# Index scores of all blocks first, three selections side by side, in a decoder with four parallel mixers

## Chip, core and metric

The kernel runs on one core of a Trainium2 chip. The metric is the device time of one launch in microseconds (us). The engines are TensorE (PE; its weight loads are PEld), VectorE (DVE), ScalarE (ACT), GpSimd (POOL) and SyncE (SP), which issues most DMAs. PE runs at one of two clock levels, 1.2 or 2.4 GHz; the granted clock of a stretch is given as a share of the higher one, so 0.5 is all of it at 1.2 GHz.

## What is computed

Two decoder layers act on 512 tokens of width 1024. Each layer normalises its input, projects it for four mixers of 256 columns each (hgrn2, DSA, NSA, mLSTM), puts their outputs side by side, projects them back, and adds the result; a cross-attention and a feed-forward part follow. The change touches the mixer DSA, which picks for every query the 128 keys with the highest index score and attends to these alone:

```python
topk = min(DSA_TOPK_MAX, l_ // 4)
...
    rel = jax.nn.relu(jnp.einsum('bthd,bsd->bhts', iqb, ik))
    score = jnp.einsum('bhts,bth->bts', rel, iwb).astype(F32)
    causal = key_pos[None, :] <= qpos[:, None]
    score = jnp.where(causal[None], score, -jnp.inf)
    _, idx = lax.top_k(score, topk)
    ...
    p = masked_softmax(s, (idx <= qpos[None, :, None])[:, None]).astype(v.dtype)
```

The index has 8 heads of 32 columns. A block is 128 queries; there are four. Block 0 sees 128 keys at most and selects nothing; blocks 1, 2 and 3 see 256, 384 and 512.

## The kernel before, in words

**Stages.** A layer has three stages, each with its own set of PSUM banks. The first holds the index and selection of DSA (`dsa`, L642), NSA with its compression (`nsa`, L1091, `nsa_cmp`, L1164), mLSTM (`ml`, L968), and the projections of all four mixers. The second, which PE opens with L716 (the sums of squares of DSA's latent), holds DSA's attention (`dsa_attn`, L707), hgrn2 (`hg`, L822), and the parts of the output projection (`out_stage`, L1287; its matmuls are those of L329 to L331 with 512 columns). The third holds cross-attention and feed-forward.

**Order.** Each of these is a generator; `weave` and `mix` take the next piece of the one that is least far on, by the costs that each piece yields and a total for each (COST). The program so written goes to a scheduler that orders the instructions of each engine once more, by its own simulation. At run time each engine takes its instructions strictly in that order: one that has to wait holds up all behind it.

**DSA's index and selection.** `index(tb)` (L665) splits a block's queries in two parts (`iqs`, written by ACT and POOL), transposes them on PE (L493, into `iqT`), and for each of 8 heads makes a score on PE (L679, one matmul of up to 512 columns), a relu on ACT (L681, `rel`, 4 buffers), and a row on DVE that adds it, weighted, to the block's scores `iacc` (L684, L685 for the first head, L688 for the others). `select(tb)` (L692) then takes 16 rounds, each of which finds the 8 largest (L696) and overwrites them with a very low number (L697, which the trace shows as a value load and a replace), and at last makes the mask `dmask` (L700) out of what was overwritten. There is one tile `iacc`, so block 2's accumulation comes after block 1's selection, and block 3's after block 2's. All transposes and scores of the index go through one PSUM bank, named `dt`, which NSA's compression and NSA's output (L1161) use as well:

```python
self.banks(banks, "ba", tp=1, sc=2, o=1, dt=1, mb=1)
...
self.alias[id(pd)] = {"tp": "dt", "sc": "dt"}
```

**What hangs on it.** When `dsa` has ended, `hg_space` (L772) closes DSA's memory and opens that of `h_v` and `h_g`, for which `hg_in` (L778) waits; these are hgrn2's last two projections, 192 matmuls of 256 columns (L339 to L341, from `proj_tok`, L476).

**Neighbours in the first stage.** mLSTM's projection chunks are copied to `m_x` (L473) and convolved in DVE rows of 512 columns (L1008, `m_y`, and L1012, `m_th`); its gates go through two scans (L984, L986, on `m_row`). For each of four heads it makes scores in bank `mb` (L1048, triples), multiplies them by a decay on DVE (L1056, `m_p`), multiplies by the values (L1065), and normalises into `mo` (L1069 to L1082, many through the helper on L351). NSA's compression gathers its input in `n_blk` and splits it in two halves of `n_bs` (L1185 and, through L351, the row after it), once for keys and once for values; PE multiplies these with streamed weights (L1192, 64x256). NSA's two attentions use bank `sc` for scores (L552) and `o` for values (L574).

Of the kernel before, what the change touches and what calls it, by code (L numbers as in the profile page):

```python
# [7 lines left out]
FT = mybir.dt.float32  # L8
FR = mybir.dt.float32r
BF = mybir.dt.bfloat16  # L10
U8 = mybir.dt.uint8
AF = mybir.ActivationFunctionType
OP = mybir.AluOpType
AX = mybir.AxisListType

D, S, MEM, DEPTH, FF = 1024, 512, 256, 2, 2816
KC = D // 128
TB = S // 128
# [3 lines left out]
NEG = -1e30  # L22
# [184 lines left out]
class Kernel:  # L207
# [434 lines left out]
    def dsa(self, pool, keep):  # L642
        nc = self.nc
        idx = self.d_idx
        st = self.t(pool, "d_st", [128, 64], bufs=1)

        ik = idx[:, :, 256:288]
        self.sumsq(st[:, 4:8], ik, pool)
        self.rsqrt(pool, st[:, 8:12], st[:, 4:8], 1.0 / 32, EPS)
        self.tt(ik, ik, st[:, 8:12, None].to_broadcast([128, TB, 32]), OP.mult)  # L650
        self.tt(ik, ik, self.row("idxk_gain")[:, None, :].to_broadcast([128, TB, 32]), OP.mult)
        self.rope(idx[:, :, 256:288].rearrange("p t (h d) -> p t h d", h=1), self.ic, self.isn, 4, pool)
        iq = idx[:, :, 0:256].rearrange("p t (h d) -> p t h d", h=8)
        self.rope(iq, self.ic, self.isn, 4, pool)
        iks = self.t2(pool, "iks", [128, TB, 96], FR)
        nc.vector.tensor_copy(iks[:, :, 0:32], ik)
        nc.vector.tensor_copy(iks[:, :, 32:64], ik)
        self.tt(iks[:, :, 64:96], ik, iks[:, :, 0:32].bitcast(FT), OP.subtract)
        ikT = self.t(pool, "ikT", [128, S], FR, bufs=1)
        self.transpose_blocks(ikT[0:96], lambda j: iks[:, j, :].bitcast(FT), TB, nc.vector.tensor_copy, rows=96,  # L660
                              pool=pool)

        yield 4.0

        def index(tb):  # L665
            n = (tb + 1) * 128
            iqs = self.t(pool, "iqs", [128, 8, 96], FR, bufs=1)
            nc.scalar.activation(iqs[:, :, 0:32], iq[:, tb], AF.Copy)
            nc.scalar.activation(iqs[:, :, 64:96], iq[:, tb], AF.Copy)
            self.tt(iqs[:, :, 32:64], iq[:, tb], iqs[:, :, 0:32].bitcast(FT), OP.subtract, nc.gpsimd)  # L670
            iqT = self.t(pool, "iqT", [128, 8, 128], FR, bufs=1)
            for g in range(2):
                self.transpose_blocks(iqT[0:96, 4 * g:4 * g + 4].rearrange("p a b -> p (a b)"),
                                      lambda j: iqs[:, 4 * g + j, :].bitcast(FT), 4, self.act_copy, rows=96,
                                      pool=pool)
            acc = self.t(pool, "iacc", [128, S], bufs=1)[:, :n]
            for h in range(8):
                sc = self.psum("sc", pool=pool)
                nc.tensor.matmul(sc[:, :n], iqT[0:96, h], ikT[0:96, :n], start=True, stop=True)  # L679
                rel = self.t2(pool, "rel", [128, S])  # L680
                nc.scalar.activation(rel[:, :n], sc[:, :n], AF.Relu, scale=1.0 / 16)  # L681
                w = idx[:, tb, 288 + h:289 + h]
                if h == 0:
                    nc.vector.tensor_scalar(acc[:, :n - 128], rel[:, :n - 128], w, None, op0=OP.mult)  # L684
                    nc.vector.scalar_tensor_tensor(acc[:, n - 128:n], rel[:, n - 128:n], w, self.k("neg"),  # L685
                                                   op0=OP.mult, op1=OP.add)
                else:
                    nc.vector.scalar_tensor_tensor(acc, rel[:, :n], w, acc, op0=OP.mult, op1=OP.add)  # L688
                yield 0.7
            return acc  # L690

        def select(tb, acc, masks):  # L692
            n = (tb + 1) * 128
            m8 = self.t(pool, "m8", [128, 8])
            for r in range(16):
                nc.vector.max(m8, acc)  # L696
                nc.vector.match_replace(acc, m8, acc, -3e38)  # L697
                yield 0.4 + 0.25 * tb
            masks[tb] = self.t(keep, f"dmask{tb}", [128, n], BF, bufs=1)
            nc.vector.tensor_scalar(masks[tb], acc, -2e38, NEG, op0=OP.is_gt, op1=OP.mult)  # L700

        masks = self.d_masks = {0: None}
        for tb in range(1, TB):
            acc = yield from index(tb)
            yield from select(tb, acc, masks)

    def dsa_attn(self, pool):  # L707
        nc, l = self.nc, self.l
# [828 lines left out]
    def run(self):  # L1537
        nc = self.nc
        late = ExitStack()
        for l in range(DEPTH):  # L1540
# [8 lines left out]
            right, index = ExitStack(), ExitStack()  # L1549
            self.hqf = self.pool(right, "hgqf", side="right")  # L1550
            self.mo = {2: self.t(self.mp, "mo2", [128, 2, S], bufs=1), 3: self.t(self.mp, "mo3", [128, TB, 256], bufs=1)}
            pd = self.pool(index, "dsa", n2=4, n4=0, side="right")
            self.alias[id(pd)] = {"tp": "dt", "sc": "dt"}
            acc = self.dsa_in(pd)
            if l == 0:
# [44 lines left out]
            with ExitStack() as e:  # L1600
                p = self.pool(e, "xa")
# [29 lines left out]
```

## Time and profile before

| | before |
|---|---|
| median of 3 runs | 1687.93 us (1684.38 to 1699.76) |
| profiled execution | 1688.9 us |
| its span | 1687.1 us |
| PE busy | 1607.5 us, 95% |
| DVE, ACT, POOL busy | 924.0, 712.5, 799.1 us |
| mean granted clock of PE | 0.972 |

The profile is of one execution. "Busy" of PE counts a matmul from start to end, at whichever clock it ran. A row of a timeline gives start, duration, engine, line, operation, tiles (output <- inputs), sizes, and in brackets the engine's idle time ahead of it and what ended that. Layer 0's first stage ends at about 268 us, layer 1's at about 1115 us.

### The profile page before, as it was taken

Reading aid. Unit: us, or ns where it says so; the run is one execution under the profiler, and the core shown is the slowest. Engines: PE = TensorE matmul, PEld = TensorE weight load, DVE = VectorE, ACT = ScalarE, POOL = GpSimd, SP = SyncE. Lnnn points to the kernel's source line nnn. Section 1 sums busy time; section 2 is a strip of 40 time slices with the busy share of each in tenths; the row PEclk is TensorE's granted clock in tenths of the full one; section 3 lists DMA queues with packets and bytes.
Section 4 is the critical chain, followed back from the end, with each engine's and each line's share of the span. In section 5 each row is a group of like instructions: output and inputs, shape, how many; then the busy total and the mean of one; then the engine's idle time right before and its main releaser. Section 6 shows DMA issues by size and latency. Waiting matters only on the chain.

```text
span 1687.1 us, 25484 instructions
## 1 busy us (share of the span) xinstructions
PE 1607.5 (95%) x9256; PEld 1333.1 (79%) x9262; DVE 924.0 (55%) x1760; ACT 712.5 (42%) x1525; POOL 799.1 (47%) x698
## 2 busy tenths in 40 slices
PE   7899998998899989999999999989998999999999
PEld 7778877777788868888898887677877888888887
DVE  5697688876755330344225884879786644123420
ACT  5555453454654443443324433423665433223321
POOL 5664333456448888874412010144672344444442
PEclk9999997999999999999999999979999999999999
DMA  5342212212338999953355734122131233333331
GB/s 160 89 119 76 70 34 84 57 38 85 112 121 286 305 316 319 333 192 93 105 156 178 262 107 132 58 95 57 45 119 38 66 97 90 92 100 94 94 103 66
DMA packets 114365, 212.72 MB, mean 126 GB/s; under 512 B 12984, under 2 KB 30136, under 8 KB 114240
## 3 DMA queue, kind: packets, MB, share of 16 engines
q1 hardware_dynamic: 111888, 206.11, 38.7%
q10 hardware_dynamic: 2032, 3.94, 0.7%
q8 instruction: 73, 1.20, 0.3%
q0 software_dynamic: 320, 1.05, 0.2%
q14 instruction: 52, 0.43, 0.1%
HBM read 170.69 MB, written 40.35 MB: 125 GB/s over the span
## 4 chain that ended last, share of the span: by engine, by line
PE 84%; DVE 8%; issue 3%; DMA 2%; POOL 2%; ACT 2%; SPq 0%; POOLq 0%; ACTq 0%; DVEq 0%
PE acc L329 14%; PE acc L331 14%; PE acc L330 14%; PE sc L330 5%; PE sc L331 5%; PE sc L329 5%; PE acc L339 3%; PE acc L340 3%; PE acc L341 3%; PE hb L856 3%; PE o L574 2%; PE sc L552 2%; PE tp L493 2%; PE mb L1048 1%; PE dt L493 1%
## 5 line engine op out<-in xcount | busy, mean ns | idle before, releaser
L293 POOL TENSOR_TENSOR wl<-wr,wh 128x512 fp32r<-128x512 f32 (+5 forms) x432 | 551.7, 1285 | 459.3 <-ACT wh L292 447.8
L292 ACT ACTIVATE wh<-wr 128x512 fp32r<-128x512 f32 (+5 forms) x432 | 252.1, 592 | 336.2 <-PE acc L330 149.2
L329 PE MATMUL acc<-xh,wh 128*128 128x512 f32 (+1 forms) x704 | 276.9, 395 | 0.8 <-ACT xh L1283 0.5
L330 PE MATMUL acc<-xl,wh 128*128 128x512 f32 (+1 forms) x704 | 274.6, 390 | 2.9 <-DVE xl L1277 2.9
L331 PE MATMUL acc<-xh,wl 128*128 128x512 f32 (+1 forms) x704 | 275.4, 392 | 0.4 <-POOL wl L293 0.4
L466 DVE TENSOR_TENSOR xT<-acc,xT 128x512 f32<-128x512 f32 (+1 forms) x112 | 68.1, 611 | 214.4 <-PE acc L331 213.6
L329 PEld LDWEIGHTS acc<-xh,wh 128*128 128x128 f32 x704 | 133.9, 191 | 32.1 <-issue 1.7
L330 PEld LDWEIGHTS acc<-xl,wh 128*128 128x128 f32 x704 | 134.3, 191 | 30.8 <-DVE xl L1277 4.0
L331 PEld LDWEIGHTS acc<-xh,wl 128*128 128x128 f32 x704 | 134.1, 190 | 28.7 <-POOL wl L293 1.1
L329 PE MATMUL acc<-f_gh,wh 128*128 128x512 f32 x352 | 139.1, 397 | 6.8 <-ACT f_gh L1491 6.8
L339 PE MATMUL acc<-wh,xh 128*128 128x256 f32 (+2 forms) x480 | 140.6, 296 | 4.9 <-DMA wh<-whl 3.8
L331 PE MATMUL acc<-f_gh,wl 128*128 128x512 f32 x352 | 139.7, 398 | 0.7 <-POOL wl L293 0.7
L330 PE MATMUL sc<-xl,wh 128*128 128x512 f32 x352 | 139.7, 397 | 0.0
L330 PE MATMUL acc<-f_gl,wh 128*128 128x512 f32 x352 | 139.5, 398 | 0.0
L340 PE MATMUL acc<-wl,xh 128*128 128x256 f32 (+2 forms) x480 | 139.0, 291 | 0.0
L331 PE MATMUL sc<-xh,wl 128*128 128x512 f32 x352 | 139.0, 395 | 0.0
L329 PE MATMUL sc<-xh,wh 128*128 128x512 f32 x352 | 138.0, 393 | 0.0
L341 PE MATMUL acc<-wh,xl 128*128 128x256 f32 (+2 forms) x480 | 137.4, 288 | 0.0
L318 POOL TENSOR_TENSOR phl<-pr,phl 128x512 fp32r<-128x512 f32 (+3 forms) x72 | 95.1, 1321 | 35.0 <-ACT phl L317 31.8
L317 ACT ACTIVATE phl<-pr 128x512 fp32r<-128x512 f32 (+3 forms) x72 | 44.2, 613 | 133.9 <-DMA pr<-in_wst 117.2
L339 PEld LDWEIGHTS acc<-wh,xh 128*128 128x128 f32 x480 | 92.9, 194 | 8.8 <-DMA wh<-whl 4.3
L340 PEld LDWEIGHTS acc<-wl,xh 128*128 128x128 f32 x480 | 93.3, 195 | 1.4 <-issue 0.8
(407 smaller groups left out, 3159.8 us busy)
## 6 DMA issues: line engine op xcount, KB each, us to landing
wr<-in_wst SPq DMA_DIRECT2D x332, 256.0 KB, 2.7
whl<-phl SPq DMA_DIRECT2D x52, 512.0 KB, 3.9
pr<-in_wst SPq DMA_DIRECT2D x52, 256.0 KB, 4.1
wh<-whl SPq DMA_DIRECT2D x52, 256.0 KB, 4.1
wl<-whl SPq DMA_DIRECT2D x52, 256.0 KB, 4.4
wr<-in_wst SPq DMA_DIRECT2D x48, 128.0 KB, 2.2
wr<-in_wst SPq DMA_DIRECT2D x32, 192.0 KB, 2.4
whl<-phl SPq DMA_DIRECT2D x8, 524.0 KB, 3.7
```

The source lines that it names most:

```text
L292: nc.scalar.activation(hi, raw, AF.Copy)
L293: nc.gpsimd.tensor_tensor(lo, raw, hi.bitcast(FT), op=OP.subtract)
L318: nc.gpsimd.tensor_tensor(both[:, 1], raw, both[:, 0].bitcast(FT), op=OP.subtract)
L329: self.nc.tensor.matmul(acc, wh, xh, start=(j == 0), stop=False)
L330: self.nc.tensor.matmul(acc, wh, xl, start=False, stop=False)
L331: self.nc.tensor.matmul(acc, wl, xh, start=False, stop=(j == n - 1))
L339: self.nc.tensor.matmul(acc, xh[:, s], wh, start=(first and j == 0), stop=False)
L340: self.nc.tensor.matmul(acc, xh[:, s], wl, start=False, stop=False)
L341: self.nc.tensor.matmul(acc, xl[:, s], wh, start=False, stop=(last and j == n - 1))
L466: self.nc.vector.tensor_add(self.xT[c][:, cols], acc, self.xT[c][:, cols])
L493: self.nc.tensor.transpose(p[:rows, j * 128:j * 128 + 128], src(j), self.ident)
L856: nc.tensor.matmul(sc[s0:s1, b + t0:b + t1], kk[po:po + 64, b + s0:b + s1], qq[po:po + 64, b + t0:b + t1], start=True, stop=True)
```

## The change

All three index passes come first, each into a tile of its own (`iacc1`, `iacc2`, `iacc3`); then 16 times a round of block 1, one of block 2 and one of block 3; then the three masks. The queries are split and transposed in two halves of four heads (`iqs` with one buffer, `iqT` with two, each half the size), and the pool's buffers for `rel` go from 4 to 3. In the new code lines from L665 on have other numbers: score L682, accumulation L687 to L691, maximum L700, replace L701, mask L706, and all that lies behind it stands one line further down (L1193 for L1192, L717 for L716).

```diff
+        accs = {tb: self.t(pool, f"iacc{tb}", [128, (tb + 1) * 128], bufs=1) for tb in range(1, TB)}
+
         def index(tb):
             n = (tb + 1) * 128
-            iqs = self.t(pool, "iqs", [128, 8, 96], FR, bufs=1)
...
-            iqT = self.t(pool, "iqT", [128, 8, 128], FR, bufs=1)
+            acc = accs[tb]
             for g in range(2):
...
-            acc = self.t(pool, "iacc", [128, S], bufs=1)[:, :n]
-            for h in range(8):
...
-        def select(tb, acc, masks):
-            n = (tb + 1) * 128
-            m8 = self.t(pool, "m8", [128, 8])
-            for r in range(16):
-                nc.vector.max(m8, acc)
-                nc.vector.match_replace(acc, m8, acc, -3e38)
+
+                four = iq[:, tb, 4 * g:4 * g + 4]
+                iqs = self.t(pool, "iqs", [128, 4, 96], FR, bufs=1)
+                nc.scalar.activation(iqs[:, :, 0:32], four, AF.Copy)
+                nc.scalar.activation(iqs[:, :, 64:96], four, AF.Copy)
+                self.tt(iqs[:, :, 32:64], four, iqs[:, :, 0:32].bitcast(FT), OP.subtract, nc.gpsimd)
+                iqT = self.t(pool, "iqT", [128, 4, 128], FR, bufs=2)
...
+                for h in range(4 * g, 4 * g + 4):
+                    sc = self.psum("sc", pool=pool)
+                    nc.tensor.matmul(sc[:, :n], iqT[0:96, h % 4], ikT[0:96, :n], start=True, stop=True)
+                    rel = self.t2(pool, "rel", [128, S])
...
+                    yield 0.7
+
+        for tb in range(1, TB):
+            yield from index(tb)
+
+        for r in range(16):
+            for tb in range(1, TB):
+                m8 = self.t(pool, f"m8{tb}", [128, 8])
+                nc.vector.max(m8, accs[tb])
+                nc.vector.match_replace(accs[tb], m8, accs[tb], -3e38)
                 yield 0.4 + 0.25 * tb
-            masks[tb] = self.t(keep, f"dmask{tb}", [128, n], BF, bufs=1)
-            nc.vector.tensor_scalar(masks[tb], acc, -2e38, NEG, op0=OP.is_gt, op1=OP.mult)
-
         masks = self.d_masks = {0: None}
         for tb in range(1, TB):
-            acc = yield from index(tb)
-            yield from select(tb, acc, masks)
+            masks[tb] = self.t(keep, f"dmask{tb}", [128, (tb + 1) * 128], BF, bufs=1)
+            nc.vector.tensor_scalar(masks[tb], accs[tb], -2e38, NEG, op0=OP.is_gt, op1=OP.mult)
...
-            pd = self.pool(index, "dsa", n2=4, n4=0, side="right")
+            pd = self.pool(index, "dsa", n2=3, n4=0, side="right")
```

What the scheduler makes of it shows in the order of the built programs. On PE, in layer 0, a score of block 3 (`dt<-ikT,iqT 128x512`) stood among the projections' matmuls of 512 columns before. Here is the first of the eight:

```order
L330 MATMUL acc<-xl,wh 128x512
L679 MATMUL dt<-ikT,iqT 128x512
L331 MATMUL acc<-xh,wl 128x512
L329 MATMUL acc<-xh,wh 128x512
L330 MATMUL acc<-xl,wh 128x512
L331 MATMUL acc<-xh,wl 128x512
L329 MATMUL acc<-xh,wh 128x512
```

Now the eight stand in this place, ahead of NSA's first compressed keys (`n_hid`):

```order
L493 MATMUL dt<-kc,iqs 96x128 x4
L574 MATMUL o<-PT,n_tok 64x128 x4
L682 MATMUL dt<-ikT,iqT 128x512
L993 MATMUL mb<-kc,m_row 128x4 x4
L682 MATMUL dt<-ikT,iqT 128x512 x2
L993 MATMUL mb<-kc,m_row 128x4 x4
L682 MATMUL dt<-ikT,iqT 128x512
L493 MATMUL dt<-kc,iqs 96x128 x4
L682 MATMUL dt<-ikT,iqT 128x512 x4
L1201 MATMUL dt<-kc,n_hid 128x64 x2
L521 MATMUL tp<-kc,qd 128x128 x4
L1209 MATMUL dt<-n_w_1098,n_hT 128x64 x2
```

All eight scores of block 3 follow one another within seven rows, with transposes and 128x4 matmuls of mLSTM's gates between them, and eleven rows further down begins NSA's second compression (L1193). Before, the eight were spread over some 150 rows.

On DVE, in layer 0, block 1's last rounds, its mask (`dmask`) and the second pass of `n_bs`, which PE's second compression reads, stood so:

```order
L697 MATCH_REPLACE iacc<-m_830,iacc 128x256
L351 TENSOR_TENSOR n_blk<-n_blk,cols 128x16x31
L696 MAX m_830<-iacc 128x8
L1185 CAST n_bs<-n_blk 128x16x32
L697 MATCH_REPLACE iacc<-m_830,iacc 128x256
L351 TENSOR_TENSOR n_bs<-n_blk,n_bs 128x16x32
L700 TENSOR_SCALAR dmask_1180<-iacc 128x256
L473 TENSOR_TENSOR m_x<-acc,R 128x512
```

And now so, where `iacc_571` is block 2's tile and `iacc_572` is block 3's:

```order
L691 SCALAR_TENSOR_TENSOR iacc_572<-rel,d_idx,iacc_572 128x512
L700 MAX m_1923<-iacc_571 128x8
L1013 SCALAR_TENSOR_TENSOR m_th<-m_th,m_y 128x512
L351 TENSOR_TENSOR n_blk<-n_blk,cols 128x16x31
L700 MAX m_1371<-iacc_572 128x8
L701 MATCH_REPLACE iacc_571<-m_1923,iacc_571 128x384
L351 TENSOR_TENSOR ql<-tp,qh 128x512
L1211 COPY n_cmp_1323<-dt 128x64
L1186 CAST n_bs<-n_blk 128x16x32
L701 MATCH_REPLACE iacc_572<-m_1371,iacc_572 128x512
L700 MAX m_2012<-iacc_571 128x8
L351 TENSOR_TENSOR n_bs<-n_blk,n_bs 128x16x32
```

The row that finishes `n_bs` has moved from one row ahead of block 1's mask to 55 rows behind it (that mask is 45 rows ahead of the first row shown); conv rows, accumulations of blocks 2 and 3 and rounds of both now stand between.

On PE, at the end of layer 0's first stage, mLSTM's last head stood so before:

```order
L1048 MATMUL mb<-m_hi_2749,m_hi_2803 128x512
L1048 MATMUL mb<-m_lo,m_hi_2803 128x512
L1048 MATMUL mb<-m_hi_2749,m_lo 128x512
L1048 MATMUL mb<-m_hi_2749,m_hi_2803 128x384
L1048 MATMUL mb<-m_lo,m_hi_2803 128x384
L1048 MATMUL mb<-m_hi_2749,m_lo 128x384
L1161 MATMUL dt<-n_eT,n_vbd 128x512
L1048 MATMUL mb<-m_hi_2749,m_hi_2803 128x256
L1048 MATMUL mb<-m_lo,m_hi_2803 128x256
L1048 MATMUL mb<-m_hi_2749,m_lo 128x256
L1048 MATMUL mb<-m_hi_2749,m_hi_2803 128x128
L1048 MATMUL mb<-m_lo,m_hi_2803 128x128
L1048 MATMUL mb<-m_hi_2749,m_lo 128x128
```

Now, for two of its triples:

```order
L1049 MATMUL mb<-m_hi_2800,m_hi_2859 128x384
L1049 MATMUL mb<-m_lo,m_hi_2859 128x384
L1049 MATMUL mb<-m_hi_2800,m_lo 128x384
L329 MATMUL acc<-xh,wh 128x512
L330 MATMUL acc<-xl,wh 128x512
L331 MATMUL acc<-xh,wl 128x512
L329 MATMUL acc<-xh,wh 128x512
L330 MATMUL acc<-xl,wh 128x512
L331 MATMUL acc<-xh,wl 128x512
L1049 MATMUL mb<-m_hi_2800,m_hi_2859 128x256
L1049 MATMUL mb<-m_lo,m_hi_2859 128x256
L1049 MATMUL mb<-m_hi_2800,m_lo 128x256
```

Before, nothing but one matmul of NSA stood among the triples of L1048; now matmuls of the output stage (512 columns) stand between them, and hgrn2's projections (256 columns) ahead of them. In all 144 matmuls of 256 columns and 12 of 512 that stood behind the second stage's first matmul (L716, now L717) in layer 0 stand ahead of it now, and 96 and 12 in layer 1.

## Rows read from the trace of the kernel before

**Rows 1.** The page, part 1: busy time of each engine, share of the span, instructions.

```profile
PE 1607.5 (95%) x9256; PEld 1333.1 (79%) x9262; DVE 924.0 (55%) x1760; ACT 712.5 (42%) x1525; POOL 799.1 (47%) x698
```

**Rows 2.** Table by stretches: length, busy us by engine, granted clock, DMA share, GB/s.

```profile
240.00:275.00 35.00, 26.98 (x162) 20.01 (x162) 32.55 (x84) 10.73 (x27) 3.09 (x3) 0.74 0.03 8
275.00:310.00 35.00, 31.22 (x213) 28.00 (x212) 28.43 (x53) 12.95 (x27) 22.34 (x28) 0.87 0.40 124
1085.00:1110.00 25.00, 17.62 (x112) 14.64 (x110) 24.66 (x66) 6.28 (x16) 1.34 (x2) 0.74 0.00 1
1110.00:1130.00 20.00, 16.21 (x117) 15.75 (x117) 12.18 (x20) 5.65 (x12) 12.32 (x18) 0.82 0.56 185
110.00:130.00 20.00, 16.21 (x125) 14.37 (x125) 19.90 (x32) 11.59 (x28) 13.39 (x9) 0.91 0.49 146
310.00:410.00 100.00, 99.68 (x768) 82.48 (x770) 72.74 (x149) 50.05 (x129) 54.95 (x61) 1.00 0.18 52
950.00:970.00 20.00, 18.95 (x146) 16.19 (x145) 16.00 (x37) 8.75 (x23) 0.73 (x1) 0.91 0.77 263
1130.00:1250.00 120.00, 119.06 (x881) 98.09 (x883) 96.42 (x197) 59.48 (x152) 68.03 (x72) 1.00 0.20 58
```

**Rows 3.** PE's timeline, end of layer 0's first stage: start, us, operation, [idle <-releaser].

```profile
258.77 2.08 PE L1161 MATMUL dt<-n_eT,n_vbd 128*128 128x512 f32 x2 [0.69 <-DVE mo L351]
...
272.57 1.08 PE L1281 MATMUL tp<-kc,mo 128*128 128x128 f32 x4 [2.54 <-DVE mo L351]
```

**Rows 4.** DVE's timeline in the same stretch: block 3's rounds and its mask.

```profile
266.06 0.69 DVE L696 MAX8 m<-iacc 128x8 f32<-128x512 f32 x1
...
267.58 0.69 DVE L696 MAX8 m<-iacc 128x8 f32<-128x512 f32 x1
...
274.08 0.43 DVE L700 TENSOR_SCALAR dmask<-iacc 128x512 bf16<-128x512 f32 x1
```

**Rows 5.** PE's timeline, 291 to 297.5 us: first and last of 43 matmuls.

```profile
291.89 0.28 PE L339 MATMUL acc<-wh,xh 128*128 128x256 f32 x1
...
296.86 0.28 PE L339 MATMUL acc<-wh,xh 128*128 128x256 f32 x1
```

**Rows 6.** DVE's timeline, 110 to 118 us: n_bs, block 1's mask, mlstm's scans.

```profile
110.51 1.35 DVE L351 TENSOR_TENSOR n_bs<-n_blk,n_bs 128x512 fp32r<-128x512 f32 x1
111.78 0.28 DVE L700 TENSOR_SCALAR dmask<-iacc 128x256 bf16<-128x256 f32 x1
...
114.52 1.18 DVE L984 TENSOR_TENSOR_SCAN m_row<-one,m_row 4x512 f32<-4x512 f32 x1
...
117.47 2.17 DVE L986 TENSOR_TENSOR_SCAN m_row<-zero,m_row 4x512 f32<-4x512 f32 x1
```

**Rows 7.** Tile view of iacc: durations ns min/median/max, first and last start, forms.

```profile
L696 DVE MAX8 m<-iacc x96: 397/561/696, 79.5 to 1108.4; 128x8 f32<-128x256 f32 x32, 128x8 f32<-128x384 f32 x32, 128x8 f32<-128x512 f32 x32
L697 DVE MATCH_VALUE_LOAD iacc<-m,iacc x96: 60/92/93, 82.1 to 1109.1; 128x8 f32 x96
L697 DVE MATCH_REPLACE8 iacc<-m,iacc x96: 397/543/678, 82.2 to 1109.2; 128x256 f32<-128x256 f32 x32, 128x384 f32<-128x384 f32 x32, 128x512 f32<-128x512 f32 x32
L688 DVE SCALAR_TENSOR_TENSOR iacc<-rel,d_idx,iacc x42: 466/742/1772, 54.9 to 1078.4; 128x256 f32<-128x256 f32 x14, 128x384 f32<-128x384 f32 x14, 128x512 f32<-128x512 f32 x14
```

**Rows 8.** Line view of L1008, mlstm's convolution (columns as in rows 7).

```profile
L1008 DVE SCALAR_TENSOR_TENSOR m_y<-m_x,cols,m_y x24: 731/752/1872, 122.2 to 1065.9; 128x512 f32<-128x512 f32 x24
```

**Rows 9.** PE's timeline, 64 to 67 us: two scores of block 1.

```profile
64.86 0.28 PE L679 MATMUL dt<-ikT,iqT 96*128 96x256 f32 x1
...
66.21 0.28 PE L679 MATMUL dt<-ikT,iqT 96*128 96x256 f32 x1
```

**Rows 10.** Tile view of rel: what ScalarE's relu waited for (us, times).

```profile
  PE dt L679: 30.5, 20
```

**Rows 11.** PE's timeline: second stage's first matmul, and hgrn2's last transposes.

```profile
268.23 1.81 PE L716 MATMUL dt<-one,ckvsq 128*128 128x1 f32 x8
...
414.54 0.69 PE L1281 MATMUL tp<-kc,h_g 128*128 128x128 f32 x2 [2.17 <-DVE h_g L351]
```

More of the change, by code (lines that the diff above doesn't have):

```diff
@@ L663, in dsa @@
         yield 4.0
+        accs = {tb: self.t(pool, f"iacc{tb}", [128, (tb + 1) * 128], bufs=1) for tb in range(1, TB)}
         def index(tb):
             n = (tb + 1) * 128
-            iqs = self.t(pool, "iqs", [128, 8, 96], FR, bufs=1)
-            nc.scalar.activation(iqs[:, :, 0:32], iq[:, tb], AF.Copy)
-            nc.scalar.activation(iqs[:, :, 64:96], iq[:, tb], AF.Copy)
-            self.tt(iqs[:, :, 32:64], iq[:, tb], iqs[:, :, 0:32].bitcast(FT), OP.subtract, nc.gpsimd)
-            iqT = self.t(pool, "iqT", [128, 8, 128], FR, bufs=1)
@@ L672, in index @@
-            for g in range(2):
-                self.transpose_blocks(iqT[0:96, 4 * g:4 * g + 4].rearrange("p a b -> p (a b)"),
-                                      lambda j: iqs[:, 4 * g + j, :].bitcast(FT), 4, self.act_copy, rows=96,
-                                      pool=pool)
-            acc = self.t(pool, "iacc", [128, S], bufs=1)[:, :n]
-            for h in range(8):
[L678 to L689, printed above, removed]
@@ L690, in index @@
-            return acc
-        def select(tb, acc, masks):
-            n = (tb + 1) * 128
-            m8 = self.t(pool, "m8", [128, 8])
-            for r in range(16):
-                nc.vector.max(m8, acc)
-                nc.vector.match_replace(acc, m8, acc, -3e38)
+            acc = accs[tb]
+            for g in range(2):
+                four = iq[:, tb, 4 * g:4 * g + 4]
[4 more added lines that the diff above has]
+                iqT = self.t(pool, "iqT", [128, 4, 128], FR, bufs=2)
+                self.transpose_blocks(iqT[0:96].rearrange("p a b -> p (a b)"), lambda j: iqs[:, j, :].bitcast(FT), 4,
+                                      self.act_copy, rows=96, pool=pool)
+                for h in range(4 * g, 4 * g + 4):
+                    sc = self.psum("sc", pool=pool)
+                    nc.tensor.matmul(sc[:, :n], iqT[0:96, h % 4], ikT[0:96, :n], start=True, stop=True)
+                    rel = self.t2(pool, "rel", [128, S])
+                    nc.scalar.activation(rel[:, :n], sc[:, :n], AF.Relu, scale=1.0 / 16)
+                    w = idx[:, tb, 288 + h:289 + h]
+                    if h == 0:
+                        nc.vector.tensor_scalar(acc[:, :n - 128], rel[:, :n - 128], w, None, op0=OP.mult)
+                        nc.vector.scalar_tensor_tensor(acc[:, n - 128:n], rel[:, n - 128:n], w, self.k("neg"),
+                                                       op0=OP.mult, op1=OP.add)
+                    else:
+                        nc.vector.scalar_tensor_tensor(acc, rel[:, :n], w, acc, op0=OP.mult, op1=OP.add)
+                    yield 0.7
```

## Prediction

> **What bounds the kernel now.** I read the page first: TensorE (PE) is busy 95% of the span, the vector engine (DVE) 55%, ScalarE 42%, GpSimd 47% [rows 1]. So the time is PE's work plus what PE loses, and PE loses in two ways: it waits, or it runs at 1.2 instead of 2.4 GHz (a granted clock of 0.74 over 35 us is 35 x 0.26 x 2 = 18 us at the lower level). The table by stretches [rows 2] shows where. In the long middles (as 310 to 410 and 1130 to 1250 us) PE is full and at 2.4 GHz. It loses where the first stage of a layer ends: 8.0 of 35 us idle at 240 to 275 and 3.8 more up to 310, then in layer 1 7.4 of 25 us at 1085 to 1110 and 3.8 more up to 1130. In the same stretches DVE is 93% and 99% busy. The timelines say with what: PE stands at matmuls that wait for DVE to make nsa's and mlstm's outputs (mo) [rows 3], and on DVE the rounds of block 3's selection (maximum, value load, replace: 1.52 us from one maximum to the next) stand between these rows, until the mask is made at 274.08 us [rows 4]. The stall is short of covering work, too: hgrn2's projections, which are free of all this, stand behind it in PE's order.
>
> **What the change moves.** The order of the built program shows three things.
>
> First, block 3's selection leaves the end. Its mask is made some 100 DVE rows earlier, and 48 triples of hgrn2's projection matmuls (144) and 12 matmuls of the output stage now stand in front of the matmul L717 that opens the second stage, as fill between mlstm's last scores. By the spacing of such matmuls (0.118 us for 256 columns, 42 of them from the first row to the last [rows 5], and twice that for 512) that is 144 x 0.118 + 12 x 0.23 = 19.8 us of PE work; in layer 1 96 and 12, 14.1 us.
>
> Second, a new stall comes into the middle of the first stage. The eight scores of block 3 follow one another in PE's order with nearly nothing between, and the next matmuls of any length, nsa's second compression (L1193), read n_bs, which DVE now makes 55 rows behind dmask of block 1, where before it stood just ahead of that mask (110.51 and 111.78 us [rows 6]). PE takes its matmuls in order, so it can't pass L1193 before DVE has gone through those rows. Their sum in layer 0, by the rows of before: two accumulations of 384 columns at 0.60 (between the least, 0.47, and the median, 0.74) and eight of 512 at 0.74: 7.1; 13 selection instructions of block 2 at 0.56 (maximum) and 0.63 (load and replace) and one round of block 3 at 1.52: 9.2 [rows 4, 7]; six of conv's m_y at 0.75 [rows 8], and two m_th at 0.7 as an estimate from these: 5.9; mlstm's two scans at 1.2 and 2.2 [rows 6] with three more rows of 512 columns at 0.67: 5.4; nsa's n_blk, n_bs, ql, n_hs and small rows, an estimate from n_bs: 7.5. Together 35.1, less 0.08 us each because a row starts before the one ahead has ended (110.51 + 1.35, next at 111.78 [rows 6]): 56 x 0.08 = 4.5. So some 30 us. PE's own work in that stretch, counted from the order (from block 2's seventh score to L1193) at the spacings above and at 0.15 us for a transpose, is 10 us with its waits for hand-overs. PE loses about 21 us. At 110 to 130 it lost 3.8 us before, and some 1.5 us to the clock [rows 2]; hence 16 us more. After such a wait PE restarts at 1.2 GHz, as it does behind the stall at the stage's end (clock 0.87 over 275 to 310 [rows 2]): 3 us of work at that level takes 1.5 us more. In layer 1 the mask of block 1 stands behind the last accumulation of block 2, so the stretch is 41 rows and 22 us by the same prices, PE's work in it 8 us, and 950 to 970 lost some 2 us before: 12 us more, and 1.5 at the restart.
>
> Bounds of the stall. Below: were DVE free, a score would only wait for its bank, which ScalarE's relu has to empty; the closest two scores of before are 1.35 us apart [rows 9], eight are 11 us, no more than PE's own work and what it lost there before. Above: the conv and accumulate rows reach 1.77 and 1.87 us when GpSimd works beside them, while the selection rows never pass 0.70 [rows 7, 8]; 15 such rows at 1 us more make it 15 us longer in layer 0, where GpSimd is 67% busy at 110 to 130, and nothing in layer 1, where it is 4% [rows 2]. I take the value without it, since a PE that stands still frees no weight buffers and gives GpSimd little to split.
> The Trainium skill ("Perfetto Trace Analysis", section "Optimizing Tensor Performance") wants independent matmul groups to rotate through PSUM banks so that the emptying of one overlaps the next. These 24 scores have one bank, before and after; the trace agrees so far that ScalarE's relu waited 20 times for a score [rows 10]. By the rule alone the new stall would be the 11 us of the lower bound, which is the second rival.
>
> Third, stage two begins later and with less fill. L717 comes 20 us of moved work plus the new stall later, less what the end of stage one gives back. Behind it stand fewer matmuls by just the moved 19.8 us, so PE as such loses nothing; but the chains of hgrn2 and of dsa's attention (146 us from 268.23 to 414.54 [rows 11]) ran beside those matmuls, and DVE has 73 to 97 us of work in each 100 to 120 us of it [rows 2]. Where the shorter stretch is too short for the chain, PE waits. Between nothing (the chain shrinks as PE's queue does) and all of 19.8 + 14.1 = 34 us I take 5, near the lower end, because PE, not DVE, was the full engine there.
>
> **Small parts, costed at nothing.** iqs and iqT are made in halves: 12 more ScalarE and 6 more GpSimd instructions, each of half the size, on engines 42% and 47% busy [rows 1]. Three relu buffers in place of four: accumulation h - 3 instead of h - 4 must be done before relu h; in the early blocks it was. If that cover is gone, it lies inside the new stall, which DVE sets anyway. The count of DVE and PE instructions is the same. No DMA is added.
>
> **The sum, against the profiled execution (1688.9 us; its span is 1687.1, the median of the runs 1687.93).** Layer 0: new stall +16, restart +1.5. End of stage one: 240 to 310 lost 8.0 + 3.8 idle, and of 27 us at 1.2 GHz (0.74 and 0.87 [rows 2]) some 16 were busy, 8 us too many: 20 in all. What stays: the last head's scores, mask multiplies and the transposes that wait for mo are still a chain, with 39 fills of 0.12 to 0.23 us between; I keep 6 us. So -14. Layer 1: +12, +1.5; 11.2 idle and 20 us at 1.2 GHz, 9 of them busy, 4.5: 16 in all, 4 stay: -12. Less fill in stage two: +5. Sum: 16 + 1.5 - 14 + 12 + 1.5 - 12 + 5 = +10. I go to 1700, a point above, as the new stalls are counted row by row while what the stage's end gives back is estimated.
>
> **Rivals.** (a) Slower: stage two is bound by its chain. Place: PE at hb, sc and dt matmuls between L717 and the transposes of h_g. It decides from the point where PE is idle there for over 10% of the stretch. For it: the chain starts some 30 us later in layer 0 and keeps its DVE work of 100 us. Against: PE was 99.7% busy at 310 to 410 [rows 2], so the chain had waited for PE. Price: half of the 34 us instead of 5, +12, and with the GpSimd contention in the first stall another 8: 1720. (b) Faster: the new stall is only the bank's hand-over (11 us, hidden by PE's work and what was lost there before), and the end of both stages gives back its 26 us: +3 - 26 + 5 = -18, 1671. For it: the rows counted in front of n_bs need not start late; those that wait for nothing on PE (conv, block 2's rounds) may run while PE is still at work ahead of the scores. Against: DVE was 99.5% busy at 110 to 130 already [rows 2], so it has no time in hand there. (c) The selections don't run side by side as the words say: block 1's sixteen rounds are through before block 2's first, and only blocks 2 and 3 alternate. That is what the order shows; the time still depends on where the rounds stand, not on their turns, so this alone is 1689.
>
> **Chances.** The forecast, 1700 with a range of its own from 1689 to 1712: 0.50. Rival (a): 0.21. Rival (b): 0.22. Rival (c): 0.07. About 1% (17 us) is what a measurement of this kernel can tell from no change. Slower by more than that, over 1705: most of (a), 0.18, and three tenths of the forecast, 0.15: 0.33. Faster, under 1671: half of (b) and what lies beyond it, 0.14. The rest, 0.53, lies within 1%. The range from 1669 to 1721 leaves out a tenth at either end: the outer halves of (a) and of (b).
>
> **What would show it.** Right: a dip of PE and of its clock at some 115 to 145 and 950 to 980 us with DVE full, the eight scores of block 3 there one accumulation apart, block 3's mask at about 185 instead of 274 us, fill matmuls between mlstm's last scores, and the dips at 255 to 275 and 1090 to 1110 mostly gone. Wrong: no dip in the middle (then (b)), or the dips at the end gone and PE idle by over 10 us more between L717 and h_g's transposes (then (a)).

## The result and the profile after

| | before | after |
|---|---|---|
| median | 1686.66 us (4 runs) | 1709.97 us (4 runs, 1704.78 to 1718.87) |
| ratio of the two | | 1.014 (95% interval 1.0109 to 1.0172) |
| profiled execution, its span | 1688.9, 1687.1 us | 1713.6, 1711.8 us |
| mean granted clock of PE | 0.972 | 0.961 |

The change makes the kernel 1.4% slower; its profiled execution is 3.6 us above its median. The page, part 1, which answers to [rows 1], shows PE 14 us busier although its work is the same: part of it ran at the lower clock. DVE is 14 us less busy.

```profile
PE 1621.5 (95%) x9256; PEld 1340.7 (78%) x9262; DVE 910.4 (53%) x1760; ACT 715.1 (42%) x1537; POOL 799.9 (47%) x704
```

The table by stretches of the kernel after, as [rows 2] for before (length, busy us of PE, PEld, DVE, ACT, POOL, granted clock, DMA share, GB/s):

```profile
100.00:160.00 60.00, 45.23 (x281) 33.43 (x280) 59.01 (x145) 34.74 (x86) 28.27 (x24) 0.77 0.26 78
160.00:298.00 138.00, 137.55 (x930) 113.99 (x928) 69.70 (x153) 61.12 (x134) 50.23 (x39) 1.00 0.23 65
298.00:340.00 42.00, 35.75 (x194) 28.49 (x193) 35.87 (x74) 13.33 (x30) 23.00 (x28) 0.96 0.33 105
340.00:375.00 35.00, 35.00 (x177) 29.46 (x177) 22.98 (x55) 9.14 (x25) 11.14 (x15) 0.56 0.03 8
375.00:429.00 54.00, 52.32 (x461) 43.65 (x463) 38.60 (x84) 31.42 (x84) 32.97 (x37) 1.00 0.14 40
955.00:1000.00 45.00, 32.41 (x167) 21.92 (x166) 43.91 (x102) 22.43 (x55) 6.38 (x8) 0.66 0.20 64
1100.00:1147.00 47.00, 46.93 (x355) 40.45 (x355) 17.05 (x32) 19.49 (x44) 14.05 (x11) 1.00 0.22 74
1147.00:1170.00 23.00, 18.22 (x91) 14.99 (x91) 20.02 (x43) 6.44 (x12) 13.12 (x21) 0.78 0.38 126
```

There are two dips in the middle of the first stages (100 to 160, 955 to 1000), with DVE full. The ends of these stages (160 to 298, 1100 to 1147) are without any loss now. The second stage of layer 0 has 35 us in which PE is never idle and yet runs at 1.2 GHz nearly throughout (340 to 375).

Put as losses, where a loss is PE's idle time plus, for each us, busy time times (1 - granted clock):

| stretch (us in before; after) | before | after | change |
|---|---|---|---|
| layer 0, start (0 to 100; 0 to 100) | 21.4 | 22.1 | +0.7 |
| first stage's middle (100 to 160; same) | 5.5 | 22.5 | +17.0 |
| its rest (160 to 268.2; 160 to 298.0) | 9.3 | 0.4 | -8.9 |
| second stage (to 414.5; to 429.1) | 16.9 | 24.8 | +7.9 |
| third stage, start of layer 1 (to 889.6; to 922.3) | 21.8 | 18.1 | -3.7 |
| layer 1, first stage's middle (120 us each) | 7.5 | 24.1 | +16.6 |
| its rest (to 1114.6; to 1147.3) | 12.2 | 0.1 | -12.1 |
| second stage (to 1244.2; to 1268.9) | 6.8 | 12.6 | +5.8 |
| rest | 15.9 | 15.0 | -0.9 |

The sum, +22.4, is most of the 24.7 us by which the spans differ.

What PE waits for in the new dip is in its timeline of layer 0 (columns as in [rows 3]; the last three rows are of the second stage):

```profile
117.58 0.49 PE L682 MATMUL dt<-ikT,iqT 96*128 96x512 f32 x1 [0.32 <-ACT iqT L497]
...
125.92 0.79 PE L682 MATMUL dt<-ikT,iqT 96*128 96x512 f32 x1 [0.68 <-ACT iqT L497]
127.40 0.79 PE L682 MATMUL dt<-ikT,iqT 96*128 96x512 f32 x1 [0.69 <-ACT rel L684]
129.45 0.80 PE L682 MATMUL dt<-ikT,iqT 96*128 96x512 f32 x1 [1.26 <-ACT rel L684]
131.00 0.80 PE L682 MATMUL dt<-ikT,iqT 96*128 96x512 f32 x1 [0.76 <-ACT rel L684]
132.48 0.47 PE L1201 MATMUL dt<-kc,n_hid 64*128 64x64 f32 x2 [0.69 <-ACT rel L684]
137.64 1.09 PE L521 MATMUL tp<-kc,qd 128*128 128x128 f32 x4 [4.69 <-DVE n_hs L351]
...
143.94 1.12 PE L574 MATMUL o<-PT,n_tok 128*64 128x128 f32 x8 [0.23 <-ACT PT L497]
144.85 1.07 PE L605 MATMUL tp<-kc,stat 128*64 128x128 f32 x8
145.85 0.48 PE L1193 MATMUL acc<-wh,n_bs 128*64 128x256 f32 x1
...
297.99 1.00 PE L717 MATMUL dt<-one,ckvsq 128*128 128x1 f32 x8
...
339.60 0.39 PE L552 MATMUL sc<-kst,qh 128*128 128x256 f32 x1 [0.95 <-ACT P L560]
...
429.08 0.38 PE L1282 MATMUL tp<-kc,h_g 128*128 128x128 f32 x2
```

A score takes 0.79 us at 1.2 GHz, then PE waits 0.69 us until ScalarE's relu has emptied the bank, then comes the next: 1.48 us a score, against which a matmul of that size among others takes 0.23 us of PE ([rows 5], twice the spacing). The eight and the transposes between them fill 117.6 to 132.5. The longest wait follows, 4.69 us for DVE, at the transposes of qd, NSA's queries (L521); the profile puts it down to n_hs, and the row ahead of n_hs makes qd itself. Of the 14.6 us of waits that the timeline lists between 100 and 160 us, 4.9 are for a relu that empties the bank, 1.0 for iqT, 6.9 for DVE (n_hs, 1.59 at m_row, 0.66 at spread) and 1.8 for NSA's softmax on ScalarE (P, PT).

At L1193, where the prediction put the stall, PE doesn't wait at all. DVE's timeline shows why: the row that finishes n_bs is made 2.0 us before PE gets there. It shows, too, what the wait at L521 was: from 105.15 us on no row of DVE has an idle time noted ahead of it (31.7 of 32.0 us busy from 105.66 to 137.63), and qd and n_hs stand behind these rows. Block 3's mask, 274.08 us in [rows 4], is there at 185.22:

```profile
105.15 1.37 DVE L691 SCALAR_TENSOR_TENSOR iacc<-rel,d_idx,iacc 128x384 f32<-128x384 f32 x1 [0.51 <-ACT rel L684]
...
134.66 2.58 DVE L1181 COPY n_blk<-n_kv 64x496 f32<-64x496 f32 x2
137.27 0.23 DVE L1128 COPY qd<-n_qr 128x128 f32<-128x128 f32 x1
137.41 0.22 DVE L351 TENSOR_TENSOR n_hs<-dt,n_hs 128x64 f32<-128x64 f32 x1
...
143.16 0.67 DVE L351 TENSOR_TENSOR n_bs<-n_blk,n_bs 128x512 fp32r<-128x512 f32 x1
...
185.22 0.43 DVE L706 TENSOR_SCALAR dmask<-iacc 128x512 bf16<-128x512 f32 x1
```

In the kernel before, the same row of qd stood ahead of block 1's mask (111.78 us [rows 6]):

```profile
106.84 0.23 DVE L1127 COPY qd<-n_qr 128x128 f32<-128x128 f32 x1
```

The tile view of rel, which answers to [rows 10], has 26 waits of the relu for a score in place of 20, and below them the scores that wait for a relu:

```profile
  PE dt L682: 30.7, 26
...
  PEld dt L682: 16.8, 14
  PE dt L682: 11.2, 12
```

The last three rows of PE's timeline answer to [rows 11]: the second stage runs from 297.99 to 429.08 us, 131.1 us in place of 146.3. The wait at 339.60 is the last before the clock falls; none follows while it is low.

### The profile page after: what moved, and what is told of

The parts are those of the page before. It is cut to its first block, busy times and chain, and to the rows that moved or that the text cites. A ratio compares the mean times of both kernels' runs of the same rounds, so it can differ in the third digit from the quotient of the medians.

```text
span 1711.8 us, 25529 instructions
## 1 busy us (share of the span) xinstructions
PE 1621.5 (95%) x9256; PEld 1340.7 (78%) x9262; DVE 910.4 (53%) x1760; ACT 715.1 (42%) x1537; POOL 799.9 (47%) x704
## 3 DMA queue, kind: packets, MB, share of 16 engines
q10 hardware_dynamic: 2032, 3.94, 0.7%
## 4 chain that ended last, share of the span: by engine, by line
PE 67%; DVE 8%; POOL 2%; ACT 2%; issue 2%; DMA 1%; SPq 0%; POOLq 0%; ACTq 0%; DVEq 0%
PE acc L329 12%; PE acc L330 12%; PE acc L331 12%; PE sc L330 5%; PE sc L331 5%; PE sc L329 5%; PE acc L339 2%; PE acc L340 2%; PE acc L341 2%; PE hb L857 2%; PE tp L493 1%; PE o L574 1%; PE sc L552 1%; PE mb L1049 1%; PE acc L1193 1%
## 5 line engine op out<-in xcount | busy, mean ns | idle before, releaser
L293 POOL TENSOR_TENSOR wl<-wr,wh 128x512 fp32r<-128x512 f32 (+5 forms) x432 | 546.1, 1273 | 487.8 <-ACT wh L292 458.7
L331 PE MATMUL acc<-xh,wl 128*128 128x512 f32 (+1 forms) x704 | 271.4, 386 | 0.0
```

The source lines that it names most:

```text
L293: nc.gpsimd.tensor_tensor(lo, raw, hi.bitcast(FT), op=OP.subtract)
L331: self.nc.tensor.matmul(acc, wl, xh, start=False, stop=(j == n - 1))
```

## The experiments

The theory after the first trace: scores that stand close together in PE's order pass through their one bank at the pace of a score and a relu, and PE, which takes its matmuls in order, can do nothing else meanwhile; and the second stage, with 20 us of fill taken out of it, loses PE's clock. The rivals: DVE's queue sets the pace of the stall; the turns of the rounds cost; the small parts cost. All ratios are against the kernel before, run beside; the losses are those of each version's profiled execution.

**E1, selections one after another.** All index passes first, then each block's 16 rounds and its mask.

```diff
-        for r in range(16):
-            for tb in range(1, TB):
...
+        def select(tb):
...
+            for r in range(16):
...
+            yield from index(tb)
+        for tb in range(1, TB):
+            yield from select(tb)
```

> The changed kernel, but each block's 16 rounds and its mask come in one piece, block after block; all index passes still come first. Theory (where the scores of block 3 stand sets the time, not the turns of the rounds): within 0.4% of the changed kernel, 1704 to 1716 us, with the same stalls at 115 to 145 and 960 to 1000 us. Rival (taking the rounds in turn is what costs): back to 1684 to 1692 us.

Measured: 1711.44 us, 1.0143 (1.0094 to 1.0193); 22.5 and 22.0 us lost in the two middles. The theory's number: the turns of the rounds are worth nothing.

**E2, the small parts alone.** The kernel before with `iqs` and `iqT` in halves and three buffers for `rel`.

```diff
-            iqs = self.t(pool, "iqs", [128, 8, 96], FR, bufs=1)
+                iqs = self.t(pool, "iqs", [128, 4, 96], FR, bufs=1)
...
-            pd = self.pool(index, "dsa", n2=4, n4=0, side="right")
+            pd = self.pool(index, "dsa", n2=3, n4=0, side="right")
```

> The kernel before (one tile for the scores, index and selection block by block) with the queries split in halves of four heads and three relu buffers. Theory: these small parts cost nothing, 1682 to 1692 us, no stall at 115 to 145 us. Rival (three relu buffers or the halves hold PE up): over 1697 us.

Measured: 1687.57 us, 1.0008 (0.999 to 1.0025). They cost nothing.

**E3, two banks for the scores.** The changed kernel, with DSA's scores in the two banks of NSA's.

```diff
-            self.alias[id(pd)] = {"tp": "dt", "sc": "dt"}
+            self.alias[id(pd)] = {"tp": "dt"}
```

> The changed kernel with DSA's scores in the two banks that NSA's scores use in place of the one bank they share with NSA's compression; the transposes stay where they were. If the one bank sets the pace of block 3's scores (1.48 us each: a score at 1.2 GHz and a relu), the loss at 100 to 160 us falls from 22 to under 10 us and the time to 1685 to 1697 us. If DVE's queue does (DVE 100% busy there), the loss stays over 16 us and the time at 1702 to 1715 us.

Measured: 1673.51 us, 0.9917 (0.9896 to 0.9939), below both expected ranges and faster than the kernel before. Its table by stretches and two of block 3's scores in PE's timeline:

```profile
100.00:160.00 60.00, 56.85 (x413) 47.25 (x412) 59.77 (x143) 35.37 (x84) 37.60 (x29) 1.00 0.40 116
```

```profile
103.64 0.39 PE L682 MATMUL sc<-ikT,iqT 96*128 96x512 f32 x1
103.86 0.28 PE L1193 MATMUL acc<-wh,n_bs 128*64 128x256 f32 x1
103.98 0.39 PE L682 MATMUL sc<-ikT,iqT 96*128 96x512 f32 x1
```

DVE is busy 59.8 of 60 us, more than in the stall, and PE loses 3.2 us, so a full DVE by itself doesn't hold PE up. The two scores shown start 0.34 us apart, with no wait for a relu. But with the other bank the scheduler also wrote another order: the eight scores stand at 84.7 to 116.0 us, most of them apart, and on DVE qd and the second n_bs, for which the prediction and the trace of the changed kernel had PE waiting, are made 21 and 20 us earlier:

```profile
116.10 0.23 DVE L1128 COPY qd<-n_qr 128x128 f32<-128x128 f32 x1
...
123.64 0.67 DVE L351 TENSOR_TENSOR n_bs<-n_blk,n_bs 128x512 fp32r<-128x512 f32 x1
```

So bank, place of the scores and DVE's order changed together here.

**E4, index of block 3 behind selection 1.** Separate tiles, one bank.

```diff
-        for tb in range(1, TB):
-            yield from index(tb)
+        yield from index(1)
+        for tb in range(1, TB):
+            if tb < TB - 1:
+                yield from index(tb + 1)
+            yield from select(tb)
```

> Separate tiles, but index of block 3 is written behind the selection of block 1 (index 1, index 2, selection 1, index 3, selection 2, selection 3). In PE's order four of block 3's scores stand where all eight stood, four some 30 us of PE work later; the second stage's first matmul stands within 1.5 us of PE work of where the change put it. Theory (packing the scores makes the stall): the new stalls halve, 17 and 20 us to about 8 each, and the time is 1685 to 1697 us. Rival (the second stage with less fill is what costs): 1702 to 1715 us.

Measured: 1683.43 us, 0.9986 (0.997 to 1.0001). The middles lose 11.5 and 10.9 us where the changed kernel lost 22.5 and 24.1. Against the kernel before (5.5 and 7.5) the stall is 6.0 and 3.4 us in place of 17.0 and 16.6: more than half of it goes, in the same single bank. The time is a little under the theory's range. The halving that the theory wanted was not tested, as the trace has no four scores together. In layer 0 block 3's first four stand behind the second compression, 1.6 to 6.3 us apart, the others from 171.1 to 181.8 us, and PE waits at none of them:

```profile
134.51 0.40 PE L682 MATMUL dt<-ikT,iqT 96*128 96x512 f32 x1
136.07 0.39 PE L682 MATMUL dt<-ikT,iqT 96*128 96x512 f32 x1
138.40 0.48 PE L682 MATMUL dt<-ikT,iqT 96*128 96x512 f32 x1
144.71 0.40 PE L682 MATMUL dt<-ikT,iqT 96*128 96x512 f32 x1
```

What is left in this middle is therefore not the bank's, and here, too, DVE makes qd and the second n_bs 16 us earlier than in the changed kernel (121.37 and 127.53 us).

**E5, four rounds of sixteen.** The changed kernel with a quarter of the rounds.

```diff
-                nc.vector.max(m8, accs[tb])
-                nc.vector.match_replace(accs[tb], m8, accs[tb], -3e38)
+                if r < 4:
+                    nc.vector.max(m8, accs[tb])
+                    nc.vector.match_replace(accs[tb], m8, accs[tb], -3e38)
```

> The changed kernel with 4 of the 16 rounds of each selection (12 are left out, so more keys stay selected in the sense of the mask; the rest is computed as before). PE's order around block 3's scores stays as in the changed kernel, DVE has about 13 rounds fewer in the stretch. If the single bank sets the pace, the eight scores stay 1.4 to 1.5 us apart and of the 17 and 20 us lost in the middle at least 11 stay in each layer: 1695 to 1712 us. If DVE's queue does, the scores close up, the middle loses under 8 us and the time falls to 1670 to 1688 us.

Measured: 1731.94 us, 1.0254 (1.0225 to 1.0282). The scores in PE's timeline:

```profile
127.73 0.79 PE L682 MATMUL dt<-ikT,iqT 96*128 96x512 f32 x1 [0.68 <-ACT iqT L497]
...
131.07 0.79 PE L682 MATMUL dt<-ikT,iqT 96*128 96x512 f32 x1 [0.69 <-ACT rel L684]
132.55 0.79 PE L682 MATMUL dt<-ikT,iqT 96*128 96x512 f32 x1 [0.69 <-ACT rel L684]
```

The pace, 1.48 us, and the losses of the middles, 22.3 and 21.2 us, stay, as the single bank wants; 42.8 us of DVE work stand in 100 to 160 instead of 59.0. But between 115 and 145 us mlstm's rows filled DVE even so (29.9 of 30 us), qd was made at 138.01 us, and PE waited for it 3.88 us as before. So this run doesn't tell the bank from DVE's queue. The time missed both expectations: of the 19.7 us that its span is longer than the changed kernel's, 6.7 are lost in layer 0 ahead of the second stage outside the middle, 6.7 in the rest of layer 1's first stage and 3.8 in the second stages. Why an order with less DVE work has these losses was not followed up.

**E6, hgrn2's last projection held back.** It is taken out of `hg_in` and written behind the first stage's weave, with a scale that reads mlstm's last output times zero.

```diff
+            rg = self.t(self.sp, "rg", [128, TB])
+            nc.vector.scalar_tensor_tensor(rg, self.mo[3][:, :, 255], 0.0, self.rcol, op0=OP.mult, op1=OP.add)
+            self.all(self.proj_tok("hgg", lambda tb: self.h_g[:, tb], 256, self.x, scale=rg))
             left.close()
```

> The changed kernel with hgrn2's last projection (96 matmuls of 256 columns) held back by a data dependency on mlstm's last output, so that most of it is fill for the second stage again; the first stage's middle is left as it is. PE work ahead of the second stage's first matmul falls by 8.4 us per layer. Theory (the second stage of layer 0 lost 15 us at 1.2 GHz for want of fill): its losses fall from 24.8 to 10 to 15 us, and the time to 1695 to 1704 us. Rival (the low clock there has another cause, or the fill is missed in the first stage): 1706 to 1716 us.

Measured: 1721.59 us, 1.0204 (1.0172 to 1.0235). The time missed both ranges. Half a hit in the stage itself: the 35 us at nearly half clock are gone,

```profile
340.00:375.00 35.00, 35.00 (x251) 28.25 (x248) 27.70 (x58) 16.13 (x44) 17.46 (x19) 1.00 0.19 52
```

and layer 0's second stage loses 18.6 instead of 24.8 us, more than the 10 to 15 expected, since 9.6 us of clock loss are left (16.9 before), most of it ahead of 330 us now. But the ends of the first stages lose 5.9 and 5.6 us again, where they lost 0.4 and 0.1. The fill is missed where it is taken away; moving it gains nothing.

**E7, two banks in the kernel before.** The edit of E3, made in the kernel before.

```diff
-            self.alias[id(pd)] = {"tp": "dt", "sc": "dt"}
+            self.alias[id(pd)] = {"tp": "dt"}
```

> The kernel before, with DSA's scores in the two banks of NSA's scores; nothing else is changed. If the two banks give the gain of the two-bank kernel by themselves (1673 us), 1668 to 1680 us. If the index passes have to come first as well for it, 1682 to 1692 us.

Measured: 1702.98 us, 1.0087 (1.006 to 1.0114): slower than the kernel before, which neither expectation had. Hgrn2's fill moves ahead of the second stage here too (it starts at 294.8 us in place of 268.2, of which some 10 us are more losses ahead of it and the rest is work), while block 3's selection still ends with the first stage (its mask at 271 us); the rest of that stage loses 14.7 us (9.3 before) and the second stage 19.6.

**E8, E4 and E3 together.** To the edit of E4 comes that of the banks.

```diff
-            self.alias[id(pd)] = {"tp": "dt", "sc": "dt"}
+            self.alias[id(pd)] = {"tp": "dt"}
```

> Index of block 3 behind the selection of block 1, and the scores in NSA's two banks. If both gains come from the same stall, no more than two banks alone with all index passes first: 1670 to 1678 us. If spreading block 3's scores still helps with two banks: 1660 to 1670 us.

Measured: 1688.8 us, 0.9992 (0.9967 to 1.0016), with ten runs from 1674.05 to 1692.05. A miss. The middles lose 9.2 and 6.2 us, the second stage of layer 0 25.2, of which 20.4 at the lower clock with PE busy: two banks help the middle, and this term takes it back in the execution that was profiled (1688.8 us).

**E9, added work in the second stage.** One matmul of 512 columns ahead of each group of hgrn2's products, overwritten by them.

```diff
                 sc = self.psum("hb")
+                nc.tensor.matmul(sc, self.identb, self.d_masks[3], start=True, stop=True)
```

> The changed kernel with one more matmul of 512 columns (block 3's mask times the identity, overwritten by what follows) ahead of each group of hgrn2's products: 32 per layer, some 0.2 us each at 2.4 GHz, 6.8 us of needless PE work per layer. If the 30 us at 1.2 GHz in the second stage of layer 0 come from PE having only hgrn2's short products there, the added work keeps the clock up: clock loss in that stage falls from 16.9 to under 8 us, the stage stays at 127 to 133 us, and the time is 1702 to 1716 us. If the low clock has another cause, it stays and the work comes on top: 1718 to 1728 us.

Measured: 1725.8 us, 1.0234 (1.0197 to 1.0271). The table by stretches and the added matmul in PE's timeline:

```profile
340.00:375.00 35.00, 35.00 (x254) 27.25 (x254) 29.76 (x64) 17.94 (x52) 18.27 (x22) 1.00 0.11 31
```

```profile
340.86 0.39 PE L854 MATMUL hb<-dmask,identb 128*128 128x512 bf16 x1
341.18 1.16 PE L858 MATMUL hb<-h_qs,h_k 64*128 64x128 f32 x8
```

The clock stays up: 1.7 us of clock loss in the stage instead of 16.9, and the stage takes 131.6 us with the needless work in it, against 131.1. The time still lies in the range that was meant for another cause of the low clock. An added matmul takes 0.32 us (340.86 to 341.18), not 0.2, so 64 of them are 20.5 us. Layer 0's second stage gives nearly all of its half back and layer 1's some 4 us; 8.0 us more are lost between the two, which was not followed up.

**E10, two banks, scores spread.** E3 with 1.6 for a head and half of a round's cost in the weave.

```diff
-                    yield 0.7
+                    yield 1.6
...
-                yield 0.4 + 0.25 * tb
+                yield 0.2 + 0.125 * tb
```

> Two banks for the scores, all index passes first, but the weave gives a head 1.6 instead of 0.7 and a round half of its cost, so block 3's scores stand 112 to 153 us of PE work into layer 0 instead of 62 to 85, ahead of the second stage's first matmul as before. Theory (with two banks it no longer matters where the scores stand, the selections must only be through before the first stage ends): within 0.5% of two banks alone, 1665 to 1682 us. Rival (what helped there was that all of DSA's work came early): 1684 to 1700 us.

Measured: 1670.54 us, 0.991 (0.9883 to 0.9937). As the theory has it: with two banks the scores can stand as late as 153 to 197 us. The profiled execution took 1682.8 us, more than any other of the seven.

**E11, separate tiles and two banks, block by block.** E3 with the order of the kernel before.

```diff
-        for tb in range(1, TB):
-            yield from index(tb)
...
+        def select(tb):
...
+            yield from index(tb)
+            yield from select(tb)
```

> Separate tiles and two banks, but index and selection block by block as in the kernel before: block 3's scores stand 148 to 185 us of PE work into layer 0, its selection at the first stage's end. Theory (the gain of two banks needs the selection of block 3 out of the stage's end, which only writing the index passes first does): 1690 to 1708 us, near the kernel before with two banks (1703). Rival (separate tiles are enough): 1668 to 1682 us.

Measured: 1711.91 us, 1.0139 (1.0104 to 1.0173), a little above the theory's range. Separate tiles don't give the gain; the rests of the first stages lose 17.8 and 17.7 us, and layer 0's second stage 23.4.

**E12, one bank, scores spread.** The weave costs of E10 in the changed kernel, its bank left as it is.

```diff
-                    yield 0.7
+                    yield 1.6
...
-                yield 0.4 + 0.25 * tb
+                yield 0.2 + 0.125 * tb
```

> One bank as in the changed kernel, all index passes first, with the weave costs of the spread kernel (1.6 a head, half a round): block 3's scores stand 127 to 184 us of PE work into layer 0 with 3 to 17 us of other work between two of them, and the second stage's first matmul comes 14 us of PE work earlier than in the changed kernel in layer 0. Theory (one bank costs only where the scores stand close together): the loss at 100 to 160 us is under 9 us and the time 1672 to 1690 us, since some of the stall at the first stage's end comes back. Rival (one bank costs wherever the scores stand): 1695 to 1712 us.

Measured: 1675.58 us, 0.9926 (0.9902 to 0.995). Its table by stretches, and block 3's mask in DVE's timeline:

```profile
100.00:160.00 60.00, 54.28 (x386) 46.12 (x386) 53.24 (x98) 34.88 (x88) 36.78 (x31) 0.94 0.39 111
279.00:404.00 125.00, 121.57 (x926) 100.09 (x926) 98.23 (x203) 58.46 (x149) 73.74 (x75) 1.00 0.20 63
```

```profile
269.82 0.43 DVE L706 TENSOR_SCALAR dmask<-iacc 128x512 bf16<-128x512 f32 x1
```

With the same single bank the middles lose 8.8 and 8.3 us. Block 3's scores stand from 166.9 to 228.8 us in layer 0, 3.4 to 17.7 us apart, and PE waits at none of them: a single bank costs nothing where the scores stand apart. That the middle is better says less, as it no longer holds these scores, and the second n_bs is made at 114.86 us here. The mask is as late as in before, the rest of layer 0's first stage loses 11.7 us, and yet the kernel is faster than before, as its second stage (to 403.7 us) loses 3.4 us in place of 16.9: 125 us at full clock.

## Why the prediction was right, and where it was not

**Side and size.** The time, 1710, lies in the range, near its upper end; the forecast of 1700 was too low mostly by the second stage. By its terms:

| term | predicted | measured |
|---|---|---|
| new stall, layer 0, with restart | +17.5 | +17.0 |
| new stall, layer 1, with restart | +13.5 | +16.6 |
| first stages' ends | -26 | -21.0 (-8.9 and -12.1) |
| second stages | +5 | +13.7 (+7.9 and +5.8) |
| all else | 0 | -3.9 |

The forecast counted some of the ends' gain behind L717, where the table counts it to the second stage; taken together the two terms are -21 against -7.3.

**The stall: right in size, partly by luck, and at another row.** The step "PE can't pass L1193 before DVE has gone through those rows" names the wrong row: n_bs was in time. PE was held by DVE 8 us earlier, at L521, and this wait ended the stall. DVE had next to no idle time left ahead of qd, so by this trace PE couldn't have passed L521 before 137.5 us in this order, however fast the scores had gone. In layer 1 it is the same (3.94 us, qd at 985.78 us, DVE busy 25.9 of the 26 us before).

Beside it stands a second path that the prediction thought hidden, the scores through one bank. It ends with L1201 at 132.95 us, 4.7 us ahead of DVE's; so without DVE's lateness most of the dip would, by the same trace, have been there too. The lower bound, "eight are 11 us, no more than PE's own work", took its 1.35 us from scores of 256 columns [rows 9]; for 512 at 1.2 GHz the pace is 1.48. What stands between the scores in time must stand between them in the order, and nothing did; so the 14.9 us from the first score to L1201 hide behind no other work of PE.

No run separates the two paths. Where the scores stand apart, by one bank (E4, E12) or two (E3, E10), the stall is smaller or gone, but in each of these DVE also makes the second n_bs at 114 to 128 us, not 143; E1 and E5 have neither change. So what is shown is that the stall comes and goes with the order that puts the scores together; what the bank alone costs in that order is not shown.

The size came out by two errors that nearly cancel. In layer 0's middle idle time rose by 11.0 us (3.8 to 14.8), where the prediction had 16, and the loss by the clock by 6.1 (1.7 to 7.8), where its restart had 1.5.

The Trainium skill ("Perfetto Trace Analysis", section "Optimizing Tensor Performance") wants independent matmul groups in different banks, so that one is emptied while the next is computed. In E3 the trace agrees so far that two scores start 0.34 us apart; its 3.2 us of loss in place of 22.5 come from the other order as well.

**The contention bound.** It did not come: the accumulations of block 3 in the stall took 0.72 to 0.74 us each in layer 0, and one of seven 1.75 in layer 1. In layer 0 the two copies of n_blk ahead of qd took 2.58 us, against 1.21 in layer 1; that is nearly all that the bound of 15 us came to there.

**The stages' ends** gave back 21.0 of the 26 us, by the mechanism that was named: no loss from 160 to 298 us, with fill between mlstm's scores.

**Stage two was mis-sized.** "Where the shorter stretch is too short for the chain, PE waits" priced a wait, of 5 us. What came in layer 0 was no wait, but 15.4 us of clock loss with PE busy, and E6 and E9 show on what it hangs: with needless matmuls put in, the stage's clock loss falls from 16.9 to 1.7 us, and with 8 us of fill given back to 9.6, none of it at 340 to 375 us. So rival (a) had the place right, and its sign (PE idle for over 10%) wrong: PE is idle for 7.9 of 131 us.

**Rival (c)** is settled by E1: taking the rounds in turn changes nothing. Small parts at nothing: E2.

**What beats both.** Three versions do, by 0.7 to 0.9% and by one to three lines more: two banks (E3, 0.9917), the weave's costs (E12, 0.9926), or both (E10, 0.991). What stays open is why the fall of the clock comes in some orders (the changed kernel, E1, E4, E5, E7, E8, E11; E10 in layer 1, in the one execution that was profiled) and not in others with as little fill (E3), and what starts it; why E5 is slower than the kernel with all its rounds; and how much of the stall each of its two paths would cost alone.

## What to carry to other kernels

Before matmuls of a chain are moved up, look at what stands between them in the engine's order: a group that shares one bank with its consumer runs at the pace of matmul plus emptying, and the engine that takes its work in order stands still for the sum. Then look at what the other engine has to get through before it makes the input of the next matmul behind the group: here that path was the longer one by 4.7 us. Fill that is moved from one stage to another pays in the one and is missed in the other, so price both. A busier DVE was harmless (E3: full for 60 us) where the rows that PE waits for stood early in DVE's queue and PE had other work in front of it.

## What was not expected of the hardware

PE ran at 1.2 GHz for 30 us (341 to 371 us) without any idle time, in a stretch of hgrn2's products (64x128) and short scores; ahead of it stood waits of 2.63 and 0.95 us. One matmul of 512 columns in every group of products (E9) kept the same stretch at 2.4 GHz, so there the added work of 32 matmuls of 0.32 us cost the stage 0.5 us in all.
